# A two-layer encoder trunk: top-16 one-hot steps in quarters between the other tile's searches, V's first two places in a tile of their own, the shift's product behind a fourth block

## The chip, the cores and the metric

The program runs on one core of one Trainium2 chip. The metric is the device time of one execution in microseconds (us); the median of three executions of the kernel before is 1765.74 us (1764.5 to 1771.2). One execution was recorded by the hardware profiler: it took 1761.52 us, of which 1759.8 us lie between its first and its last instruction (the span).

The engines are TensorE (PE; its weight loads are PEld), VectorE (DVE), ScalarE (ACT), GpSimd (POOL) and SyncE (SP, which here only issues DMAs). Each engine takes its instructions in the order of its own queue.

## The reference, cut to what matters

Two layers work on 272 tokens (256 and 16 meta tokens) of width 1024. Each has a token mixer (a recurrent block, then a convolution block) and behind it the block that this change touches most, an expert retrieval:

```python
def peer_block(xc, w_query, sub_keys, expert_u, expert_v):
    q = (xc @ w_query).reshape(c, PEER_HEADS, 2, PEER_HALF)
    scores = jnp.einsum('chpk,pnk->chpn', q, sub_keys)          # 128 keys on each of 2 sides
    s1, i1 = lax.top_k(scores[:, :, 0], PEER_TOPK)               # 16 of 128
    s2, i2 = lax.top_k(scores[:, :, 1], PEER_TOPK)
    cand = (s1[..., :, None] + s2[..., None, :]).reshape(c, PEER_HEADS, 256)
    s, flat = lax.top_k(cand, PEER_TOPK)                         # 16 of 256
    idx1 = jnp.take_along_axis(i1, flat // PEER_TOPK, axis=-1)
    idx2 = jnp.take_along_axis(i2, flat % PEER_TOPK, axis=-1)
    expert = idx1 * PEER_N_KEYS + idx2
    g = jax.nn.softmax(s)
    act = gelu(einsum('chkd,cd->chk', expert_u[expert], xc))
    return einsum('chkd,chk->cd', expert_v[expert], g * act)
```

After each of the two, x becomes LayerNorm(alpha * x + f(x)).

## The kernel before, in words

**Most experts are computed densely.** For all but the last few tokens the kernel multiplies x by the whole of `peer_u` (128 places of 128 experts, one 512 KB tile each) and the weighted activations by the whole of `peer_v`, instead of gathering rows. A place's fp32 weights are split in two halves, hi (ACT, L155) and lo = raw - hi (L162), and PE makes 24 matmuls for it: 16 that read hi, then 8 that read lo. Weight tiles come from SP's queue four or five places ahead; hi and lo have two buffers each.

**U1** is the first half of U (places 0 to 63, `linears` with `u_store`). For the places below `LO_FROM` = 34, POOL makes lo; from place 34 on, DVE makes it. So in the first 34 places DVE is free for the top-k. **U2** is the second half, in which the one-hot products of the gate are made too; **V** is the third loop, over the 128 places of `peer_v`.

**The top-k** (`topk_steps`) of a tile of 128 tokens is a generator of DVE work. Its steps: 16 searches of 16 among 128 (each MAX8, MAX_INDEX, MATCH_REPLACE, MAX8, MAX_INDEX: L926 to L930); the 256 sums `cand` (L933); 8 searches among 256 (L941 to L945); conversions (`s`, `pu`, `pf`, L948 to L954); a one-hot `oh` by comparison (L961), its product with the indices (L967) and a sum (L970) that yields `idx`. Both layers have two tiles. The first, the late tokens, is run at once with its one-hot steps whole (one instruction of 4096 elements each). The second (`slow`) has its 24 searches run behind the first, and its remaining steps, in halves, go between places of U1 from 34 on. All that the searches issue stands in DVE's queue ahead of DVE's first lo. A scheduler may interleave independent searches; it does so in the kernel before.

**Gathered tokens.** For a few tokens the experts are gathered by index. SP writes their positions from the first tile's `idx` to DRAM (`few_spread`, at place `SPREAD` = 21) and reads them back four places later (`few_fetch`); DVE turns them into row numbers from place 35 on (`few_ids`).

**V's weights.** V's places come in groups of `JG` = 4. `weights` splits four places' activations (ACT L271, DVE L274) into a tile `w` that shares its two buffers (tag `xs`) with the x that U2 still reads, so the first group can be written only after U2's last matmul has read x. For the first group the split goes place by place.

**The end of layer 0's V** (`collect`) finishes eight output blocks one by one. From the first two finished blocks' sum PE makes a running mean (`shift`, L865, behind the third block), ACT copies it (L866), and DVE subtracts it from all blocks (L877), while the last weights' lo (L162), the sums and the squares for the LayerNorm go on.

Of the kernel before, what the change touches and what calls it, by code (L numbers as in the profile page):

```python
# [9 lines left out]
F32R = mybir.dt.float32r  # L10
# [3 lines left out]
OP = mybir.AluOpType  # L14
# [4 lines left out]
P = 128  # L19
# [4 lines left out]
T0 = SEQ + META  # L24
HEADS = 8
# [13 lines left out]
JG = 4  # L39
JA = 64  # L40
SPREAD = 21
WROW = 256
# [22 lines left out]
class Trunk:  # L65
# [489 lines left out]
    def peer(self, layer, n, xs):  # L555
# [10 lines left out]
        with tc.tile_pool(name=f"few{layer}", bufs=1) as kp:  # L566
# [5 lines left out]
            with tc.tile_pool(name=f"top{layer}", bufs=1) as sp:  # L572
# [9 lines left out]
                for c0, md in ctiles:  # L582
                    sc = sp.tile([P, 2 * HEADS, NK], F32, tag="sc", name="sc", bufs=2)
                    for g in range(4):
                        ps = self.psum("sps", (3, 4)).rearrange("p (a b) -> p a b", a=4)
                        for i in range(4):
                            b = 4 * g + i
                            nc.tensor.matmul(ps[:, i, :], q[:, b, c0:c0 + P], self.sk[:, 2 * layer + b % 2, :],  # L588
                                             start=True, stop=True)
                        nc.scalar.activation(sc[:, 4 * g:4 * g + 4, :], ps, AF.Copy)  # L590
                    if c0:
                        picked.append((c0, md, *self.topk(sp, sc, P)))
                        for few in early + late:
                            self.few_turn(sp, few, xs)
                        for few in early:
                            if few not in near:
                                self.few_topk(sp, few, q)
                    else:
                        slow = self.topk_steps(sp, sc, P, HEADS, 2)
                        for _ in range(3 * HEADS):  # L600
                            next(slow)
                        picked.append((c0, md))

                def u_store(j, ps):
# [32 lines left out]
                    if j == SPREAD + 4:  # L637
                        with tc.issue_after(self.last_load):
                            self.few_fetch(nc.sync, near, "pos")
                    if LO_FROM < j <= LO_FROM + len(near):  # L640
                        with tc.issue_after(self.dve_lo.ins):
                            self.few_ids(near[j - LO_FROM - 1], near[j - LO_FROM - 1]["pos"])
                    if t == len(picked) and not odd:
# [9 lines left out]
            with tc.tile_pool(name=f"act1{layer}", bufs=1) as ap1:  # L653
# [124 lines left out]

                def weights(j0, count):
                    t = self.xp.tile([P, JG * 2 * T0], F32R, tag="xs", name="w")  # L780
                    t = t[:, :JG * 2 * WROW].rearrange("p (j a n) -> p j a n", j=JG, a=2)
                    w = act_a[:, j0:j0 + count, :n] if j0 < JA else act_b[:, j0 - JA:j0 - JA + count, :n]
                    for s in ((slice(jj, jj + 1) for jj in range(count)) if j0 == 0 else (slice(0, count),)):
                        self.split_x(w[:, s], t[:, s, 0, :n], t[:, s, 1, :n])
                    return [t[:, jj] for jj in range(count)]

                half = NB // 2
# [60 lines left out]
    def collect(self, sp, acc, y, n):  # L848
        nc = self.nc
        ps, take, finish_block = acc  # L850
        self.tiles(sp, n)
        xr = [take(b) for b in range(4)]
        for b in range(NB):
            self.fifth = b < NB - 1
            finish_block(b)
            self.add_squares(n)
            if b < 4:
                with self.tc.issue_after(self.dve_lo.ins):
                    xr.append(take(4 + b))
            if b == 3:  # L860
                self.sum_rest(xr[4:])
            x, p_, z = xr[b], ps[b], y[:, b, :n]
            if b == 2:
                mu = self.bank(7, "shift")
                nc.tensor.matmul(mu[:, :n], self.fours, self.total, start=True, stop=True)  # L865
                nc.scalar.activation(self.shift, mu[:, :n], AF.Copy)  # L866
            if b >= 4:
                nc.vector.tensor_tensor(self.total, self.total, p_, op=OP.add)
            nc.vector.tensor_tensor(z, x, p_, op=OP.add)
            if 0 < b < 4:  # L870
                nc.vector.tensor_tensor(self.total, y[:, 0, :n] if b == 1 else self.total, z, op=OP.add)
# [36 lines left out]

    def topk(self, sp, sc, m):
        steps = self.topk_steps(sp, sc, m, HEADS)  # L910
        while True:
            try:
                next(steps)
            except StopIteration as done:
                return done.value

    def topk_steps(self, sp, sc, m, H, parts=1):
        nc = self.nc
        K = TOPK
        sv = sp.tile([P, H, 2, K], F32, tag=f"sv{H}", name="sv", bufs=1)  # L920
        si = sp.tile([P, H, 2, K], U32, tag=f"si{H}", name="si", bufs=1)
        for b in range(2 * H):
# [6 lines left out]
            nc.vector.max(v[:, 8:16], r[:m])  # L929
            nc.vector.max_index(i[:, 8:16], v[:, 8:16], r[:m])  # L930
            yield
# [5 lines left out]
        for h in range(H):  # L937
# [6 lines left out]
            nc.vector.max(v[:, 8:16], r[:m])  # L944
            nc.vector.max_index(i[:, 8:16], v[:, 8:16], r[:m])  # L945
            yield
# [6 lines left out]
        pf = sp.tile([P, 2 * H * K, 2], F16, tag=f"pf{H}", name="pf", bufs=1)  # L953
        nc.vector.tensor_copy(pf[:m], pu[:m].rearrange("p a n -> p (a n)")[:, :, None].to_broadcast([m, 2 * H * K, 2]))  # L954
        yield
# [4 lines left out]
        for g in range(0, 2 * H, w):  # L960
            nc.vector.tensor_tensor(oh[:m, g:g + w].rearrange("p g k (a b) -> p (g k) a b", b=2),  # L961
                                    self.iota16[:m].rearrange("p (a b) -> p a b", b=2)[:, None].to_broadcast(pairs),
                                    pf[:m, g * K:(g + w) * K, None, :].to_broadcast(pairs), op=OP.is_equal)
            yield
        for g in range(0, 2 * H, w):
            s = s16[:m].rearrange("p a h k -> p (a h) k")[:, g:g + w, None, :]
            nc.vector.tensor_tensor(oh[:m, g:g + w], oh[:m, g:g + w], s.to_broadcast([m, w, K, K]), op=OP.mult)  # L967
            yield
        for g in range(0, 2 * H, w):
            nc.vector.tensor_reduce(idx[:m].rearrange("p a h k -> p (a h) k")[:, g:g + w], oh[:m, g:g + w],  # L970
                                    op=OP.add, axis=AX.X)
            yield
# [428 lines left out]
```

## Time and profile before

| What | Value |
|---|---|
| median of three executions | 1765.74 us |
| the profiled execution | 1761.52 us, span 1759.8 us |
| ACT busy | 901.4 us, 51% of the span |
| DVE busy | 1512.1 us, 86% |
| POOL busy | 625.5 us, 36% |
| mean granted PE clock | 0.994 |
| HBM | 411.35 MB read, 240 GB/s over the span |

A busy time is the sum of an engine's instructions; an idle time stands in square brackets behind the instruction that ended it, with the engine and line that released it. Idle time of an engine that nobody waits for costs nothing. The rows that the argument rests on stand in the prediction.

### The profile page before, as it was taken

How to read it: one execution, taken by the hardware profiler on the slowest of the kernel's cores; microseconds unless marked ns; L12 is line 12 of the kernel's file. 1: busy time of each engine (PE TensorE's matmuls, PEld its weight loads, DVE VectorE, ACT ScalarE, POOL GpSimd, SP SyncE). 2: the span in 40 equal slices, each digit the busy share in tenths (PEclk: the TensorE clock that was granted, in tenths of full speed). 3: DMA queues.
4: the chain of work that ended last, by engine and by line, in shares of the span. 5: the costliest groups of instructions: out<-in, count | busy, mean ns of one | idle time of the engine just before them, and what ended most of it. 6: DMA issues, size and time to landing. Idle time of an engine off the chain costs nothing.

```text
span 1759.8 us, 34693 instructions
## 1 busy us (share of the span) xinstructions
PE 1716.6 (98%) x13436; PEld 1671.8 (95%) x13436; DVE 1512.1 (86%) x2821; ACT 901.4 (51%) x1489; POOL 625.5 (36%) x424
## 2 busy tenths in 40 slices
PE   8999999999999999999998999999999999999996
PEld 7899999999999999999887899999999999999996
DVE  7786998899997899988699769988889978889875
ACT  6554545554445455885532645445445455555552
POOL 1101992211202566752000017932102117777410
PEclk9999999999999999999999999999999999999998
DMA  5546667876757999999541356579767669999983
GB/s 204 168 139 175 183 210 266 300 230 192 229 182 253 329 369 367 361 353 331 163 135 60 117 168 178 185 254 324 235 193 231 199 197 326 344 360 347 349 305 123
DMA packets 126022, 423.83 MB, mean 241 GB/s; under 512 B 20768, under 2 KB 21920, under 8 KB 125728
## 3 DMA queue, kind: packets, MB, share of 16 engines
q1 hardware_dynamic: 96272, 324.04, 55.8%
q0 software_dynamic: 29584, 97.58, 15.1%
q8 instruction: 105, 1.72, 0.4%
q14 instruction: 61, 0.50, 0.1%
HBM read 411.35 MB, written 10.20 MB: 240 GB/s over the span
## 4 chain that ended last, share of the span: by engine, by line
PE 40%; DVE 8%; DMA 1%; issue 1%; ACT 1%; POOL 1%; POOLq 0%; ACTq 0%; DVEq 0%
PE u L190 20%; PE acc L772 11%; PE acc L776 7%; DVE cy L1281 2%; DVE odd L1281 2%; DMA rows<-peer_v,ids 1%; DMA own<-own 1%; DVE lo L162 1%; PE g L697 0%; PE g L698 0%; PE sps L588 0%; PE acc L812 0%; DVE x L373 0%; DVE x L337 0%; PE var L899 0%
## 5 line engine op out<-in xcount | busy, mean ns | idle before, releaser
L155 ACT ACTIVATE hi<-raw 128x1024 fp32r<-128x1024 f32 x556 | 588.5, 1059 | 563.4 <-PE acc L772 239.1
L162 DVE TENSOR_TENSOR lo<-raw,hi 128x1024 fp32r<-128x1024 f32 x488 | 595.6, 1222 | 142.0 <-ACT hi L155 140.1
L190 PE MATMUL u<-xs,hi 128*128 128x240 f32 (+2 forms) x4544 | 568.9, 277 | 2.0 <-ACT hi L155 1.4
L190 PEld LDWEIGHTS u<-xs,hi 128*128 128x128 f32 x4544 | 537.6, 189 | 3.1 <-ACT hi L155 1.6
L772 PE MATMUL acc<-w,hi 128*128 128x416 f32 (+1 forms) x1984 | 407.9, 347 | 2.5 <-DVE w L274 1.8
L772 PEld LDWEIGHTS acc<-w,hi 128*128 128x128 f32 x1984 | 345.3, 189 | 4.3 <-DVE w L274 2.2
L1066 POOL DMA_INDIRECT rows<-peer_v,ids x128 | 206.8, 1615 | 311.6 <-DVE few_out L1107 164.9
L190 PE MATMUL u<-xs,lo 128*128 128x240 f32 (+2 forms) x2272 | 307.9, 276 | 3.6 <-POOL lo L162 3.4
L190 PEld LDWEIGHTS u<-xs,lo 128*128 128x128 f32 x2272 | 280.6, 189 | 5.7 <-POOL lo L162 5.0
L776 PEld LDWEIGHTS acc<-w,lo 128*128 128x128 f32 x2048 | 266.9, 191 | 3.7 <-DVE lo L162 2.8
L776 PE MATMUL acc<-w,lo 128*128 128x208 f32 (+1 forms) x2048 | 268.1, 272 | 1.6 <-DVE lo L162 1.6
L162 POOL TENSOR_TENSOR lo<-raw,hi 128x1024 fp32r<-128x1024 f32 x68 | 176.8, 2619 | 103.2 <-ACT hi L155 64.7
L1107 DVE SCALAR_TENSOR_TENSOR few_out<-rows,act,few_out 128x1024 f32<-128x1024 f32 x120 | 153.7, 1281 | 13.4 <-DMA rows<-peer_v,ids 13.1
L1066 POOL DMA_INDIRECT rows<-u_rows,ids x48 | 61.5, 1281 | 177.0 <-DVE rows L1073 137.4
L1083 POOL DMA_INDIRECT act<-own,turn x80 | 113.6, 1420 | 27.5 <-issue 17.7
L226 PE MATMUL u<-x,raw 128*128 128x272 f32 x480 | 113.5, 396 | 5.2 <-DMA x<-h 5.2
L226 PEld LDWEIGHTS u<-x,raw 128*128 128x128 f32 x480 | 92.2, 192 | 24.3 <-DMA raw<-w_in 5.1
L704 ACT ACTIVATE act_b<-g 128x488 f32<-128x488 f32 (+39 forms) x50 | 19.4, 389 | 122.0 <-DVE act_b L666 99.3
L381 POOL TENSOR_SCALAR xs<-x,par 128x272 fp32r<-128x272 f32 (+1 forms) x4 | 3.5, 880 | 185.6 <-DVE x L373 185.6
L679 DVE TENSOR_TENSOR AB<-iota,iT 128x2048 f16<-128x2048 f16 x50 | 61.1, 1226 | 0.0
L1073 DVE SCALAR_TENSOR_TENSOR rows<-rows,wide 128x1024 f32<-128x1024 f32 x48 | 58.5, 1219 | 1.6 <-DMA rows<-u_rows,ids 1.4
L753 POOL COPY own<-act_b 128x512 f32<-128x512 f32 (+2 forms) x15 | 14.9, 1002 | 122.2 <-ACT act_b L715 94.8
(281 smaller groups left out, 1797.7 us busy)
## 6 DMA issues: line engine op xcount, KB each, us to landing
raw<-peer_u SPq DMA_DIRECT2D x256, 512.0 KB, 4.3
raw<-peer_v SPq DMA_DIRECT2D x248, 512.0 KB, 6.4
raw<-w_query SPq DMA_DIRECT2D x28, 512.0 KB, 3.6
raw<-pw SPq DMA_DIRECT2D x22, 512.0 KB, 3.5
raw<-w_in SPq DMA_DIRECT2D x16, 512.0 KB, 4.3
raw<-w_out SPq DMA_DIRECT2D x8, 512.0 KB, 4.1
raw<-peer_v SPq DMA_DIRECT2D x16, 256.0 KB, 4.2
own<-own POOLq DMA_DIRECT2D x15, 256.0 KB, 4.9
```

What stands on the lines that cost most here:

```text
L155: self.act_hi = nc.scalar.activation(hi, raw, AF.Copy).ins
L162: i = e.tensor_tensor(lo[:, s], raw[:, s], hi[:, s].bitcast(F32), op=OP.subtract)
L190: self.mm = nc.tensor.matmul(ps[:, :n], l[:, k, :], xs(k, r)[:, :n], start=start, stop=stop)
L226: self.mm = self.nc.tensor.matmul(ps[:, :n], raw[:, k, :], x[:, k, :n], start=k == 0, stop=k == NB - 1)
L679: nc.vector.tensor_tensor(AB.rearrange("p x c (a b) -> p (x c) a b", b=2), keys, iT[:, c0 // HC].rearrange("p x c b -> p (x c) b")[:, :, N ...
L772: self.mm = nc.tensor.matmul(acc[b][:, :2 * n].rearrange("p (a t) -> p a t", a=2), hi, w[:, :, :n], start=j == 0, stop=j == NK - JG - 1, s ...
L776: self.mm = nc.tensor.matmul(main[b][:, :n], hi if p_ else lo, w[:, i, :n], start=False, stop=j == NK - 1 and not p_, skip_group_check=True)
L1066: self.last_rows = self.nc.gpsimd.indirect_dma_start(out=t, out_offset=None, in_=table, in_offset=bass.IndirectOffsetOnAxis(ap=few["ids"][ ...
L1073: self.nc.vector.scalar_tensor_tensor(t, t, 1.0, few["x"], op0=OP.mult, op1=OP.mult, accum_out=few["act"][:, k:k + 1])
L1083: self.nc.gpsimd.indirect_dma_start(out=few["act"][:, k:k + 1], out_offset=None, in_=few["table"].rearrange("p j (t o) -> (p j t) o", o=1) ...
L1107: nc.vector.scalar_tensor_tensor(few["out"], t, w, few["out"], op0=OP.mult, op1=OP.add)
L1281: nc.vector.scalar_tensor_tensor(z, h, w, z, op0=OP.mult, op1=OP.add)
```

## The change

There are three edits, and two numbers that follow from the first.

1. **One-hot steps in quarters, between searches.** The first tile's generator is now made with `parts` = 4, so each of its three one-hot steps is four instructions of 1024 elements. A new function `interleave` runs the rest of it step by step and places, after its n-th step, the second tile's searches until 4n/3 (rounded down) are done; `issue_after(step)` fixes this order, and the same chain holds the second tile's remaining eight searches behind it. `SPREAD` goes from 21 to 32 and the row numbers are made from place 38 on.
2. **V's first two places** are split into a tile `first` of their own, so they no longer share a buffer with x.
3. **In `collect`** the product for `shift` is issued behind the fourth finished block, and the sums of blocks 2 and 3 follow it.

```diff
-SPREAD = 21
+SPREAD = 32
...
-                        picked.append((c0, md, *self.topk(sp, sc, P)))
+                        quick = self.topk_steps(sp, sc, P, HEADS, 4)
+                        for _ in range(3 * HEADS):
+                            next(quick)
...
                         slow = self.topk_steps(sp, sc, P, HEADS, 2)
-                        for _ in range(3 * HEADS):
-                            next(slow)
-                        picked.append((c0, md))
+                    picked.append((c0, md))
+                picked[0] += self.interleave(quick, slow, 2 * HEADS, 3 * HEADS)
...
-                    if LO_FROM < j <= LO_FROM + len(near):
+                    if 0 <= j - SPREAD - 6 < len(near):
...
-                def weights(j0, count):
-                    t = self.xp.tile([P, JG * 2 * T0], F32R, tag="xs", name="w")
+                def weights(j0, count, t=None):
+                    if t is None:
+                        t = self.xp.tile([P, JG * 2 * T0], F32R, tag="xs", name="w")
...
+                first = first_pool.__enter__().tile([P, 2, 2, n], F32R, name="first")
...
-                    w = weights(j, JG)
+                    w = weights(j, JG) if j else weights(0, 2, first) + weights(2, 2)
...
-            if b == 2:
+            if b == 3:
                 mu = self.bank(7, "shift")
...
-            if 0 < b < 4:
-                nc.vector.tensor_tensor(self.total, y[:, 0, :n] if b == 1 else self.total, z, op=OP.add)
+            if b == 1:
+                nc.vector.tensor_tensor(self.total, y[:, 0, :n], z, op=OP.add)
             if b == 3:
+                for i in (2, 3):
+                    nc.vector.tensor_tensor(self.total, self.total, y[:, i, :n], op=OP.add)
...
+    def interleave(self, steps, others, between, count):
+        step = result = None
+        done = turns = 0
+
+        def paced(one):
+            with self.tc.issue_after(step) if step else nullcontext():
+                next(one)
+            return self.step.ins
+
+        while result is None:
+            try:
+                step = paced(steps)
+            except StopIteration as end:
+                result = end.value
+                break
+            turns += 1
+            while done < min(between, 4 * turns // 3):
+                step = paced(others)
+                done += 1
+        for _ in range(count - done):
+            step = paced(others)
+        return result
```

What this does to the queues stands at three places. **First, DVE in layer 0's top-k, around the first tile's one-hot steps.** Before (`oh` is the one-hot tile, `sc`, `sv`, `si` scores, values and indices of the second tile's searches):

```order
L967 TENSOR_TENSOR oh<-oh,s_1817 128x4096
L926 MAX sv<-sc 128x8
L970 TENSOR_REDUCE idx<-oh 128x256
L927 MAX_INDEX si<-sv,sc 128x8
L928 MATCH_REPLACE r<-sv,sc 128x128
L926 MAX sv<-sc 128x8
L929 MAX sv<-r 128x8
L927 MAX_INDEX si<-sv,sc 128x8
L930 MAX_INDEX si<-sv,r 128x8
L928 MATCH_REPLACE r<-sv,sc 128x128
```

Now, at the first quarters:

```order
L978 CAST pf<-pu 128x512
L950 MAX sv<-sc 128x8
L951 MAX_INDEX si<-sv,sc 128x8
L952 MATCH_REPLACE r<-sv,sc 128x128
L953 MAX sv<-r 128x8
L954 MAX_INDEX si<-sv,r 128x8
L985 TENSOR_TENSOR oh<-iota_98,pf 128x1024
L950 MAX sv<-sc 128x8
L951 MAX_INDEX si<-sv,sc 128x8
```

The searches moved from behind the sum to between the quarters, and a search's five instructions, which were mixed with those of its neighbour, now stand one behind the other.

**Second, DVE at the end of the same stretch, just ahead of its first lo.** Before, then now (`cand`, `fv`, `fi` belong to the second tile's searches among 256):

```order
L943 MATCH_REPLACE r_2071<-fv,cand 128x256
L944 MAX fv<-r_2071 128x8
L945 MAX_INDEX fi<-fv,r_2071 128x8
L943 MATCH_REPLACE r_2077<-fv,cand 128x256
L944 MAX fv<-r_2077 128x8
L945 MAX_INDEX fi<-fv,r_2077 128x8
L162 TENSOR_TENSOR lo<-raw,hi 128x1024
```

```order
L965 MAX fv<-cand 128x8
L966 MAX_INDEX fi<-fv,cand 128x8
L967 MATCH_REPLACE r_2086<-fv,cand 128x256
L968 MAX fv<-r_2086 128x8
L969 MAX_INDEX fi<-fv,r_2086 128x8
L162 TENSOR_TENSOR lo<-raw,hi 128x1024
```

In both, the first lo stands behind the last search; nothing of the second tile's 24 searches moved behind it.

**Third, DVE in `collect`** (`xr` and `acc` are a block's two parts, `x` their sum). Before, then now:

```order
L871 TENSOR_TENSOR total<-x_10692 128x272
L869 TENSOR_TENSOR x_10692<-xr,acc_7259 128x272
L871 TENSOR_TENSOR total<-total,x_10692 128x272
L877 TENSOR_TENSOR x_10692<-x_10692,shift 128x272 x3
L877 TENSOR_TENSOR xr<-xr,shift 128x272 x3
L869 TENSOR_TENSOR x_10692<-xr,acc_7260 128x272
L877 TENSOR_TENSOR xr<-xr,shift 128x272
L871 TENSOR_TENSOR total<-total,x_10692 128x272
L873 SCALAR_TENSOR_TENSOR total<-shift,total 128x272
L877 TENSOR_TENSOR x_10692<-x_10692,shift 128x272
L874 TENSOR_TENSOR total<-total,rest 128x272
L162 TENSOR_TENSOR lo<-raw,hi 128x1024
```

```order
L878 TENSOR_TENSOR total<-x_10706 128x272
L876 TENSOR_TENSOR x_10706<-xr,acc_7268 128x272
L876 TENSOR_TENSOR x_10706<-xr,acc_7269 128x272
L162 TENSOR_TENSOR lo<-raw,hi 128x1024
L881 TENSOR_TENSOR total<-total,x_10706 128x272
L886 TENSOR_TENSOR x_10706<-x_10706,shift 128x272
```

The last lo, which stood behind all subtractions of the shift, now stands ahead of them.

More of the change, by code (lines that the diff above doesn't have):

```diff
@@ L639, in u_store @@
                             self.few_fetch(nc.sync, near, "pos")
[L640 removed]
+                    if 0 <= j - SPREAD - 6 < len(near):
                         with tc.issue_after(self.dve_lo.ins):
[L642 removed]
+                            self.few_ids(near[j - SPREAD - 6], near[j - SPREAD - 6]["pos"])
                     if t == len(picked) and not odd:
@@ L777, in v_mm @@
                                                        stop=j == NK - 1 and not p_, skip_group_check=True)
-                def weights(j0, count):
-                    t = self.xp.tile([P, JG * 2 * T0], F32R, tag="xs", name="w")
-                    t = t[:, :JG * 2 * WROW].rearrange("p (j a n) -> p j a n", j=JG, a=2)
+                def weights(j0, count, t=None):
+                    if t is None:
+                        t = self.xp.tile([P, JG * 2 * T0], F32R, tag="xs", name="w")
+                        t = t[:, :JG * 2 * WROW].rearrange("p (j a n) -> p j a n", j=JG, a=2)
                     w = act_a[:, j0:j0 + count, :n] if j0 < JA else act_b[:, j0 - JA:j0 - JA + count, :n]
-                    for s in ((slice(jj, jj + 1) for jj in range(count)) if j0 == 0 else (slice(0, count),)):
+                    for s in ((slice(jj, jj + 1) for jj in range(count)) if j0 < JG else (slice(0, count),)):
                         self.split_x(w[:, s], t[:, s, 0, :n], t[:, s, 1, :n])
                     return [t[:, jj] for jj in range(count)]
+                first_pool = tc.tile_pool(name=f"first{layer}", bufs=1, side="right", reuse_waits="tile")
+                first = first_pool.__enter__().tile([P, 2, 2, n], F32R, name="first")
                 half = NB // 2
@@ L929, in topk_steps @@
             nc.vector.max(v[:, 8:16], r[:m])
-            nc.vector.max_index(i[:, 8:16], v[:, 8:16], r[:m])
+            self.step = nc.vector.max_index(i[:, 8:16], v[:, 8:16], r[:m])
             yield
@@ L944, in topk_steps @@
             nc.vector.max(v[:, 8:16], r[:m])
-            nc.vector.max_index(i[:, 8:16], v[:, 8:16], r[:m])
+            self.step = nc.vector.max_index(i[:, 8:16], v[:, 8:16], r[:m])
             yield
@@ L953, in topk_steps @@
         pf = sp.tile([P, 2 * H * K, 2], F16, tag=f"pf{H}", name="pf", bufs=1)
-        nc.vector.tensor_copy(pf[:m], pu[:m].rearrange("p a n -> p (a n)")[:, :, None].to_broadcast([m, 2 * H * K, 2]))
+        self.step = nc.vector.tensor_copy(pf[:m], pu[:m].rearrange("p a n -> p (a n)")[:, :, None].to_broadcast([m, 2 * H * K, 2]))
         yield
@@ L960, in topk_steps @@
         for g in range(0, 2 * H, w):
-            nc.vector.tensor_tensor(oh[:m, g:g + w].rearrange("p g k (a b) -> p (g k) a b", b=2),
+            self.step = nc.vector.tensor_tensor(oh[:m, g:g + w].rearrange("p g k (a b) -> p (g k) a b", b=2),
                                     self.iota16[:m].rearrange("p (a b) -> p a b", b=2)[:, None].to_broadcast(pairs),
@@ L966, in topk_steps @@
             s = s16[:m].rearrange("p a h k -> p (a h) k")[:, g:g + w, None, :]
-            nc.vector.tensor_tensor(oh[:m, g:g + w], oh[:m, g:g + w], s.to_broadcast([m, w, K, K]), op=OP.mult)
+            self.step = nc.vector.tensor_tensor(oh[:m, g:g + w], oh[:m, g:g + w], s.to_broadcast([m, w, K, K]), op=OP.mult)
             yield
         for g in range(0, 2 * H, w):
-            nc.vector.tensor_reduce(idx[:m].rearrange("p a h k -> p (a h) k")[:, g:g + w], oh[:m, g:g + w],
+            self.step = nc.vector.tensor_reduce(idx[:m].rearrange("p a h k -> p (a h) k")[:, g:g + w], oh[:m, g:g + w],
                                     op=OP.add, axis=AX.X)
```

8 lines of the change are left out of this document (2 added, 6 removed).

## The prediction

> **What bounds the kernel.** I read the page first, then who PE waited for, then the timelines of the three places that the change touches.
>
> ```profile
> span 1759.8 us, 34693 instructions
> PE 1716.6 (98%) x13436; PEld 1671.8 (95%) x13436; DVE 1512.1 (86%) x2821; ACT 901.4 (51%) x1489; POOL 625.5 (36%) x424
> ```
>
> PE is the bound, at 98%. A change that leaves PE's work alone can gain only what PE idles, and every microsecond that PE is made to wait is lost. PE's waits that concern this change:
>
> ```profile
> PE u L190 <- POOL lo L162: 3.4, 3, 1.4
> PE acc L772 <- DVE w L274: 1.8, 2, 0.9
> PE shift L865 <- issue: 1.7, 1, 1.7
> ```
>
> These are total, count and longest: 6.9 us together, so without side effects the change is worth some 7 us of 1760, 0.4%. Now the engine that takes the rearranged work, over the top-k of layer 0 and of layer 1 (columns: PE, PEld, DVE, ACT, POOL busy):
>
> ```profile
> 172.00:265.00 93.00, 90.99 (x804) 90.22 (x804) 91.48 (x366) 47.09 (x71) 83.84 (x32) 1.00 0.63 191
> 1064.00:1157.00 93.00, 91.53 (x810) 90.76 (x809) 88.77 (x354) 46.23 (x69) 83.45 (x32) 1.00 0.61 187
> ```
>
> DVE is busy 91.48 and 88.77 of 93 us there. It must be done with the searches when place 34 asks for its first lo, so any DVE time that the change adds soon reaches PE.
>
> **The POOL stall that the quarters are to remove.** Layer 0, the whole one-hot steps on DVE, POOL's lo beside them, and PE:
>
> ```profile
> 211.65 4.30 DVE L961 TENSOR_TENSOR oh<-iota,pf 128x4096 f16<-128x4096 f16 x1
> 216.28 4.08 DVE L967 TENSOR_TENSOR oh<-oh,s 128x4096 f16<-128x4096 f16 x1
> 220.49 4.39 DVE L970 TENSOR_REDUCE idx<-oh 128x256 f32<-128x4096 f16 x1
> 276.60 1.22 DVE L961 TENSOR_TENSOR oh<-iota,pf 128x2048 f16<-128x2048 f16 x1
> 287.38 2.28 DVE L970 TENSOR_REDUCE idx<-oh 128x128 f32<-128x2048 f16 x1
> 211.40 2.41 POOL L162 TENSOR_TENSOR lo<-raw,hi 128x1024 fp32r<-128x1024 f32 x1 [0.28 <-ACT hi L155]
> 214.09 17.95 POOL L162 TENSOR_TENSOR lo<-raw,hi 128x1024 fp32r<-128x1024 f32 x6 [0.29 <-ACT hi L155]
> 218.26 1.17 PE L190 MATMUL u<-xs,lo 128*128 128x240 f32 x8
> 222.62 1.17 PE L190 MATMUL u<-xs,lo 128*128 128x240 f32 x8 [1.41 <-POOL lo L162]
> ```
>
> With POOL idle, half the size takes 1.22 us, so the whole needs some 2.15 (doubled, less the part that the next instruction overlaps). Beside POOL it takes 4.30: it starts at 211.65, while POOL's lo runs from 211.40 to 213.81, and it ends 2.14 us after that lo. So DVE waits for POOL's running lo to end, and POOL's next one waits for DVE: six take 17.95 instead of 14.4. The sum L970 (4.39 for 4096, as against 2.28 for half) does not show it. PE's two lo groups are 4.36 apart instead of a place's 2.70 (266.09 to 268.78 below), so this costs 1.7 us, a little more with the neighbours; I take 1.9 per layer.
>
> **Searches one behind the other.** A search that is mixed with its neighbour, then dependent instructions back to back:
>
> ```profile
> 226.50 0.28 DVE L926 MAX8 sv<-sc 128x8 f32<-128x128 f32 x1
> 227.67 0.27 DVE L926 MAX8 sv<-sc 128x8 f32<-128x128 f32 x1
> 242.67 0.27 DVE L928 MATCH_REPLACE8 r<-sv,sc 128x128 f32<-128x128 f32 x1
> 242.97 0.29 DVE L929 MAX8 sv<-r 128x8 f32<-128x128 f32 x1
> 243.30 0.09 DVE L930 MATCH_VALUE_LOAD si<-sv,r 128x8 f32 x1
> ```
>
> A mixed search costs 1.17 us (226.50 to 227.67) for five instructions, about 0.20 each and 0.06 for each load. Where one reads what the one right before it wrote, the step is 0.30 and 0.33 instead of 0.20. A search has three such links, so alone it costs about 1.17 + 0.40 = 1.57.
>
> **What DVE's queue becomes, layer 0:**
> - 16 searches alone: 16 x 0.40 = **+6.4**.
> - 8 searches among 256: 24 links instead of the 12 that stand so in the tail of the order before, at the same 0.13: **+1.6**.
> - 8 quarters that contend with POOL (four of L961, four of L967), each 0.55 of its own. After a quarter POOL starts a lo of 2.41. One search later (1.57) DVE asks again and waits 0.84; after two searches (3.14) POOL is in its second lo and DVE waits 1.7. By the 4n/3 rule six quarters follow one search and two follow two: 6 x 0.84 + 2 x 1.7 + 8 x 0.55 = 12.8, against 4.30 + 4.08 = 8.4: **+4.4**. The four sums stay at 4.4 in all.
> - The two `pu` conversions now have a MAX8 between them, so each can wait for a lo of its own: 0 to 2.4, I take **+1**.
>
> Together +13.4. From both sides: if no quarter ever waited, these would take 4.4 instead of 8.4 and DVE would come out at +5; if each waited a whole lo, at +24. The quarters' wait follows from the rows above, so I stay at **+13**. In layer 1 the two `pu` stand side by side as before: **+12**.
>
> **What that does to PE.** The end of the searches, the first lo (place 34), in layer 0 a later one, and PE's use of the lo, in each layer:
>
> ```profile
> 263.24 0.42 DVE L945 FIND_INDEX8 fi<-fv,r 128x8 uint32<-128x256 f32 x1
> 264.74 1.23 DVE L162 TENSOR_TENSOR lo<-raw,hi 128x1024 fp32r<-128x1024 f32 x1 [1.07 <-ACT hi L155]
> 278.15 1.23 DVE L162 TENSOR_TENSOR lo<-raw,hi 128x1024 fp32r<-128x1024 f32 x1 [0.33 <-ACT hi L155]
> 266.09 1.06 PE L190 MATMUL u<-xs,lo 128*128 128x240 f32 x8
> 268.78 1.06 PE L190 MATMUL u<-xs,lo 128*128 128x240 f32 x8
> 1152.05 0.42 DVE L945 FIND_INDEX8 fi<-fv,r 128x8 uint32<-128x256 f32 x1
> 1156.19 1.23 DVE L162 TENSOR_TENSOR lo<-raw,hi 128x1024 fp32r<-128x1024 f32 x1 [3.72 <-ACT hi L155]
> 1160.23 1.07 PE L190 MATMUL u<-xs,lo 128*128 128x240 f32 x8
> ```
>
> In layer 0 the searches end at 263.7 and PE uses that lo at 268.8. With +13 they end at 276.7, the lo at 277.9, so PE reads it 9.1 later than now: **+9.1**. In layer 1 they end at 1152.5 + 12 = 1164.5, the lo at 1165.7 instead of a use at 1160.2: **+5.5**. The POOL stalls that vanish ahead of place 34 (1.9 and 1.9) are no further gain: PE only reaches the wait earlier. Behind place 34 DVE still idles in a place (0.33 at 278.15), so it does not fall further behind, and does not give anything back either, since PE is the bound again.
>
> SP: the spread now stands ahead of the 34th weight tile and waits for `idx`, by the same count near 256 in layer 0. That load then comes some 6 us late, as the one at place 22 does now without a wait of PE, and its hi and lo would still be done before DVE's. Nothing added. The row numbers are made three places later, five places ahead of their first product: hidden.
>
> **The clock behind a long wait.** These are windows right behind a POOL stall and behind the two longest idle stretches of PE (the clock is the third column from the end):
>
> ```profile
> 223.00:226.00 3.00, 3.00 (x30) 3.00 (x29) 3.00 (x10) 1.36 (x3) 3.00 (x2) 1.00 0.00 0
> 970.00:975.00 5.00, 5.00 (x15) 3.35 (x14) 2.74 (x8) 2.71 (x8) 0.00 (x0) 0.58 0.00 0
> 864.00:866.00 2.00, 2.00 (x15) 2.00 (x14) 1.82 (x5) 1.32 (x4) 0.00 (x0) 0.74 0.54 217
> 866.00:868.00 2.00, 2.00 (x12) 2.00 (x11) 1.97 (x7) 2.00 (x5) 0.00 (x0) 0.50 0.00 0
> ```
>
> After 6.89 us idle the granted clock is 0.58 over 5 us (2.1 us lost), after 1.73 idle 0.74 and 0.50 over 2 us each (1.5 lost). After the POOL stall of 1.41 it stays 1.00. The new waits in front of place 34 are 11 and 7 us (9.1 and 5.5, and 1.9 each by which PE comes earlier), so I add **+1.7** in each layer, 3.4. The Trainium skill (TensorE: Matmul & The Clock Gate, Part 1) says that the clock falls to half after a window of about 3.4 us of idling and comes back after one of work; by it an estimate of 1.7 us is lost behind each long wait, which agrees, but the drop behind 1.73 us would not be expected, and there the rows decide.
>
> **V's first places:**
>
> ```profile
> 545.74 1.06 ACT L155 ACTIVATE hi<-raw 128x1024 fp32r<-128x1024 f32 x1 [1.31 <-PE u L190]
> 547.53 1.80 PE L772 MATMUL acc<-w,hi 128*128 128x416 f32 x8 [0.93 <-DVE w L274]
> 1439.51 1.66 PE L772 MATMUL acc<-w,hi 128*128 128x384 f32 x8 [0.90 <-DVE w L274]
> ```
>
> PE waits 0.93 (layer 1: 0.90) for the first w. With `first` ready early, it still needs this hi, which ends at 546.80, 0.2 behind the start of the wait: gain **0.7** per layer, **-1.4**. ACT and DVE do the same instructions a place earlier, where ACT idles for 1 to 2 us.
>
> **The shift:**
>
> ```profile
> 862.90 0.44 DVE L871 TENSOR_TENSOR total<-x 128x272 f32<-128x272 f32 x1
> 863.44 0.70 PE L865 MATMUL shift<-total,fours 128*128 128x272 f32 x2 [1.73 <-issue]
> 868.96 1.22 DVE L162 TENSOR_TENSOR lo<-raw,hi 128x1024 fp32r<-128x1024 f32 x1
> 870.24 0.48 PE L776 MATMUL acc<-w,lo 128*128 128x208 f32 x2 [0.69 <-DVE lo L162]
> ```
>
> PE waits 1.73 for the sum that DVE ends at 863.3. A block's 6 matmuls (0.7) now fill part of it, so about 1.0 is left. PE waits again at 870.24 for the last lo, which is now ahead of DVE's subtractions and can be done near 865. The least is 0.7, the most what lies between (0.7 + 0.7 + 1.5 of clock, and a share of DVE's 4 us): 4. I take **-2.5**; the squares, which come after the subtractions, set the end there.
>
> **Sum:** 9.1 + 5.5 + 3.4 - 1.4 - 2.5 = **+14.1 us**. Against the profiled execution, 1761.5, that is 1775.6; the median is 4.2 above that execution, so **1780 us**, 0.8% slower. A measurement of this kernel can tell about 0.5% (8.8 us) from no change.
>
> **Rivals.**
> - *The quarters slip between POOL's lo's, and DVE stays in time* (the change does what it is built for). Against it: DVE's 4.30 for 2.15 of work. The waits go: 3.8 of POOL, 1.4, 2.5: 7.7 less, **1758**. It decides if DVE's queue grows by less than 3.9 us in layer 0 (the 1.07 idle, and 2.8 between the lo's end at 265.97 and its use at 268.78). For it: the lower bound of +5 above comes near that. 8%.
> - *DVE grows by about half*: the links cost, the waits for POOL are half of mine, +8 and +7. PE loses 4 + 0.5 and some clock (2), and gains 3.9: **1768**, inside 0.5%. 17%.
> - *Each contention rounds up to one more lo of POOL* in both layers (2.4 + 0.3 each): **1785**, as the forecast otherwise. 15%.
>
> The rule behind the first and third is on a page, too: the Trainium skill (SBUF — State Buffer, Who interferes with whom) says that a DVE instruction with two SBUF inputs and a GpSimd one that reads SBUF lock each other out for a whole instruction, whoever starts first, and that a reduction never contends; the rows above agree (4.30 and 4.39). By that rule, more and shorter instructions mean more waits for a whole lo, which speaks against this change.
>
> **How the numbers follow.** The forecast (1780) 60%, the rivals 8, 17 and 15. The range reaches from the half case, less 2, to the rounded case, plus 2: 1766 to 1787. Slower by over 0.5%: 60 + 15, less 2 that falls inside: 0.73; within 0.5%: 17 + 2 and a share of the first rival: 0.21; faster: 0.06.
>
> **What would show it.** Right: PE waits in front of place 34 in both layers, for DVE lo, 11 and 7 us; the searches end near 277 and 1165; quarters at 0.6 to 2.3 us each; no POOL stall over 0.5; a clock near 0.6 behind those waits. Wrong: a first DVE lo that still waits for ACT hi, or quarters at 0.6 throughout. PE's waits for w and shift shrink in either case.

## The result and the profile after

The changed kernel takes **1775.49 us** (median of 8 runs, 1772.58 to 1778.99), the kernel before 1765.05 us beside it (8 runs). The ratio is 1.0060, 95% interval 1.0046 to 1.0075: slower by 10.4 us. The profiled execution has a span of 1775.1 us, 15.3 more than the one before; about 4 us of that is scatter of another stage, as the last experiment shows.

The page's first lines, and those of PE's waits that concern the change, by who ended them (total, count, longest, in us):

```profile
span 1775.1 us, 34708 instructions
PE 1720.1 (97%) x13436; PEld 1673.6 (94%) x13436; DVE 1527.7 (86%) x2839; ACT 901.0 (51%) x1489; POOL 613.4 (35%) x424
```

```profile
PE u L190 <- DVE lo L162: 14.4, 2, 8.5
PE shift L872 <- PE acc L777: 1.0, 1, 1.0
PE u L190 <- POOL lo L162: 0.6, 1, 0.6
```

The waits that the change was aimed at have shrunk: for POOL's lo 3.4 to 0.6, for V's first w 1.8 to nothing, for the shift 1.7 to 1.0. One row that was not there before is larger than all of them together: 14.4 us in two waits for DVE's lo. Both stand in front of place 34. The timeline of the changed kernel shows DVE's last search, its first lo, and PE, in layer 0 and then in layer 1 (start, duration, then in brackets the idle time before it):

```profile
275.57 0.42 DVE L969 FIND_INDEX8 fi<-fv,r 128x8 uint32<-128x256 f32 x1
275.91 1.21 DVE L162 TENSOR_TENSOR lo<-raw,hi 128x1024 fp32r<-128x1024 f32 x1
277.17 2.06 PE L190 MATMUL u<-xs,lo 128*128 128x240 f32 x8 [8.54 <-DVE lo L162]
279.03 2.98 PE L190 MATMUL u<-xs,hi 128*128 128x240 f32 x16
281.85 1.06 PE L190 MATMUL u<-xs,lo 128*128 128x240 f32 x8
282.75 1.96 PE L190 MATMUL u<-xs,hi 128*128 128x240 f32 x16
...
1173.45 0.42 DVE L969 FIND_INDEX8 fi<-fv,r 128x8 uint32<-128x256 f32 x1
1173.78 1.21 DVE L162 TENSOR_TENSOR lo<-raw,hi 128x1024 fp32r<-128x1024 f32 x1
1175.04 2.06 PE L190 MATMUL u<-xs,lo 128*128 128x240 f32 x8 [5.87 <-DVE lo L162]
1176.90 2.90 PE L190 MATMUL u<-xs,hi 128*128 128x240 f32 x16
```

The first lo has no bracket: hi was ready, and DVE came to it straight from the last search. Before, that lo still waited 1.07 us for ACT's hi. Behind the wait, 8 lo and 16 hi matmuls take 2.06 and 2.98 us instead of 1.06 and 1.96, which is a cost of its own. The granted clock (third column from the end) of these stretches:

```profile
277.00:279.00 2.00, 1.83 (x8) 1.83 (x9) 1.93 (x7) 1.06 (x1) 0.00 (x0) 0.50 0.31 70
279.00:283.00 4.00, 4.00 (x29) 4.00 (x28) 2.72 (x8) 1.32 (x2) 1.04 (x1) 0.73 0.77 244
1175.00:1177.00 2.00, 1.96 (x9) 1.96 (x10) 1.97 (x6) 1.06 (x1) 0.00 (x0) 0.50 0.41 98
```

Now what DVE does on the way there, in the timeline of layer 0: POOL's lo, quarters, and two searches of each kind that follow one another.

```profile
215.77 2.52 POOL L162 TENSOR_TENSOR lo<-raw,hi 128x1024 fp32r<-128x1024 f32 x1 [0.29 <-ACT hi L155]
217.53 1.31 DVE L985 TENSOR_TENSOR oh<-iota,pf 128x1024 f16<-128x1024 f16 x1
218.45 5.10 POOL L162 TENSOR_TENSOR lo<-raw,hi 128x1024 fp32r<-128x1024 f32 x2 [0.17 <-ACT hi L155]
221.90 2.20 DVE L985 TENSOR_TENSOR oh<-iota,pf 128x1024 f16<-128x1024 f16 x1
...
229.64 0.28 DVE L950 MAX8 sv<-sc 128x8 f32<-128x128 f32 x1
231.21 0.28 DVE L950 MAX8 sv<-sc 128x8 f32<-128x128 f32 x1
232.79 2.09 DVE L991 TENSOR_TENSOR oh<-oh,s 128x1024 f16<-128x1024 f16 x1
...
268.33 0.43 DVE L968 MAX8 fv<-r 128x8 f32<-128x256 f32 x1
270.57 0.43 DVE L968 MAX8 fv<-r 128x8 f32<-128x256 f32 x1
```

The quarter at 217.53 ends 0.55 us after POOL's lo (215.77 + 2.52 = 218.29): it waited 0.76 and then worked. A search among 128 takes 1.57 us from one MAX8 to the next, one among 256 takes 2.24. Grouped over the stretch from the first quarter to the end of the searches (behind the count the total in us and the mean in ns):

```profile
L985 DVE TENSOR_TENSOR oh<-iota,pf 128x1024 f16<-128x1024 f16 x4 | 6.3, 1568 | 0.0
L991 DVE TENSOR_TENSOR oh<-oh,s 128x1024 f16<-128x1024 f16 x4 | 6.0, 1504 | 0.0
L994 DVE TENSOR_REDUCE idx<-oh 128x64 f32<-128x1024 f16 x4 | 4.8, 1200 | 0.0
```

The eight quarters take 12.3 us where the two whole steps took 8.4 (4.30 + 4.08). The Trainium skill (SBUF — State Buffer, Who interferes with whom) says that a DVE instruction with two SBUF inputs and a GpSimd one that reads SBUF exclude each other for a whole instruction. The rows agree: each quarter ends about 0.55 us after a lo of POOL, and the sums, with one input, take 1.20 each beside the same POOL work.

The other two edits, in the changed kernel's timeline:

```profile
558.48 0.83 PE L773 MATMUL acc<-first,hi 128*128 128x416 f32 x3 [0.15 <-ACT tmp L719]
877.50 0.70 PE L872 MATMUL shift<-total,fours 128*128 128x272 f32 x2 [0.97 <-PE acc L777]
```

V's first wait fell from 0.93 to 0.15 in layer 0, and in layer 1 from 0.90 to nothing.

### The profile page after: what moved, and what is told of

It reads as the page before. It is cut to its first block, busy times and chain, and to the rows that moved or that the text cites. A ratio compares the mean times of both kernels' runs of the same rounds, so it can differ in the third digit from the quotient of the medians.

```text
span 1775.1 us, 34708 instructions
## 1 busy us (share of the span) xinstructions
PE 1720.1 (97%) x13436; PEld 1673.6 (94%) x13436; DVE 1527.7 (86%) x2839; ACT 901.0 (51%) x1489; POOL 613.4 (35%) x424
## 4 chain that ended last, share of the span: by engine, by line
PE 37%; DVE 13%; issue 1%; ACT 1%; POOLq 0%; POOL 0%; DVEq 0%; ACTq 0%
PE u L190 17%; PE acc L773 11%; PE acc L777 7%; DVE cy L1305 2%; DVE odd L1305 2%; DVE lo L162 1%; PE g L698 1%; PE g L699 1%; DVE si L954 1%; DVE si L951 1%; DVE r L952 0%; DVE sv L953 0%; DVE fi L969 0%; PE pre L246 0%; DVE fi L966 0%
## 5 line engine op out<-in xcount | busy, mean ns | idle before, releaser
L773 PE MATMUL acc<-w,hi 128*128 128x416 f32 (+1 forms) x1952 | 401.6, 347 | 1.6 <-ACT hi L155 1.1
L773 PEld LDWEIGHTS acc<-w,hi 128*128 128x128 f32 x1952 | 339.9, 189 | 3.4 <-ACT hi L155 1.5
L190 PE MATMUL u<-xs,lo 128*128 128x240 f32 (+2 forms) x2272 | 309.6, 278 | 15.1 <-DVE lo L162 14.4
L1090 POOL DMA_INDIRECT rows<-peer_v,ids x128 | 199.9, 1561 | 321.4 <-DVE few_out L1131 166.1
L777 PEld LDWEIGHTS acc<-w,lo 128*128 128x128 f32 x2016 | 261.9, 191 | 7.4 <-DVE lo L162 6.4
L777 PE MATMUL acc<-w,lo 128*128 128x208 f32 (+1 forms) x2016 | 264.4, 273 | 3.4 <-DVE lo L162 3.3
```

What stands on the lines that cost most here:

```text
L190: self.mm = nc.tensor.matmul(ps[:, :n], l[:, k, :], xs(k, r)[:, :n], start=start, stop=stop)
L773: self.mm = nc.tensor.matmul(acc[b][:, :2 * n].rearrange("p (a t) -> p a t", a=2), hi, w[:, :, :n], start=j == 0, stop=j == NK - JG - 1, s ...
L777: self.mm = nc.tensor.matmul(main[b][:, :n], hi if p_ else lo, w[:, i, :n], start=False, stop=j == NK - 1 and not p_, skip_group_check=True)
L1090: self.last_rows = self.nc.gpsimd.indirect_dma_start(out=t, out_offset=None, in_=table, in_offset=bass.IndirectOffsetOnAxis(ap=few["ids"][ ...
```

## The experiments

Stage lengths below are read from PE's timeline, from one marked matmul to another. "U1" here is the part of U1 in which the one-hot steps and place 34 lie: its first 57 places, from its first matmul to PE's first transpose of top-k results (`tps`). Before, it takes 156.62 us in layer 0 and 156.05 in layer 1, in the changed kernel 165.29 and 161.99.

### Which edit loses the time

**The kernel before with the two edits of V and of the shift only:** the top-k stays as it was.

```diff
+                first = first_pool.__enter__().tile([P, 2, 2, n], F32R, name="first")
...
-                    w = weights(j, JG)
+                    w = weights(j, JG) if j else weights(0, 2, first) + weights(2, 2)
...
-            if b == 2:
+            if b == 3:
...
```

> The kernel before with V's first two places in a tile of their own and the shift behind the fourth block; the one-hot steps stay whole. Theory (these two edits are gains, the loss is all in the top-k): PE waits 0.2 instead of 0.9 for the first w in both layers and the end of layer 0's V is 2.3 us shorter, so 3.7 us less than before, about 1761; no wait of PE for a DVE lo at place 34. Rival (one of these two edits is why PE waited 3.3 us in all for a DVE lo within layer 0's V after the change): V of layer 0 is some 4 us longer here too, and the kernel is no faster than before.

Measured: 1761.59 us against 1763.87 (12 and 23 runs), ratio 0.9987, interval 0.9973 to 1.0000. That is 2.3 us faster, with an interval that just reaches no change. Layer 0's V up to the shift takes 320.97 us here, 5 more than in the first profile of the kernel before, as the rival said; the last experiment finds nearly as much without any edit. U1 is as before (156.61 and 156.75), with POOL's stalls still in it:

```profile
PE u L190 <- POOL lo L162: 4.1, 4, 1.4
```

**The changed kernel without those two edits:** only the interleaving is left.

```diff
-                    w = weights(j, JG) if j else weights(0, 2, first) + weights(2, 2)
+                    w = weights(j, JG)
...
-            if b == 3:
+            if b == 2:
...
```

> The kernel before with the quarters between the searches alone (and the later spread). Theory: the whole loss is here: PE waits about 8.5 and 5.9 us for the first DVE lo of the two layers, and the time is that of the whole change plus the 3.7 us of the other two edits, 1779. Rival (the parts depend on one another): within 1 us of the whole change, 1775, or below.

Measured: 1782.58 us (4 runs) against 1763.87, ratio 1.0097, interval 1.0073 to 1.0120; 3.6 us more than expected. U1 takes 165.04 and 162.33, like the changed kernel's, and in front of place 34 PE waits 8.5 and 5.9 us for DVE's lo, as there:

```profile
PE u L190 <- DVE lo L162: 14.7, 3, 8.5
```

So the whole loss is in the interleaving, and the other two edits give a little back.

### The chain of searches, or the quarters

**The searches hang on the quarter only, not on one another.** The quarters stay where they are; between two quarters the scheduler is free to mix independent searches.

```diff
-                step = paced(others)
+                paced(others)
...
-            step = paced(others)
+            paced(others)
```

> The whole change, but each search is ordered behind the quarter only and no longer behind the search before it, so searches mix with their neighbours again; the quarters stay between them. Theory (back-to-back dependent searches make DVE late): two searches fit into one lo of POOL (2.34 against 2.41), a turn takes 2.96, DVE's searches end 8 us sooner, PE's waits in front of place 34 fall from 8.5 and 5.9 to 0.5 and 0, and with the clock 16 us go: about 1760. PE waits for POOL's lo 0.5 in place of 1.4. Rival (the waits of eight quarters for POOL make DVE late, however the searches stand): the quarters still take 1.3 to 2.2 each, PE's waits fall by 2 us each, about 1771.

Measured: **1755.77 us** against 1763.87, ratio 0.9948, interval 0.9932 to 0.9963. This is faster than both kernels, and 4 us under what was expected. U1 takes 154.96 and 154.15 us. The waits in front of place 34 are gone; the quarters (grouped), POOL's stalls, and the end of the searches in the timeline:

```profile
L985 DVE TENSOR_TENSOR oh<-iota,pf 128x1024 f16<-128x1024 f16 x4 | 6.4, 1601 | 0.0
L991 DVE TENSOR_TENSOR oh<-oh,s 128x1024 f16<-128x1024 f16 x4 | 5.8, 1451 | 0.0
```

```profile
PE u L190 <- POOL lo L162: 0.9, 2, 0.5
```

```profile
264.26 0.42 DVE L969 FIND_INDEX8 fi<-fv,r 128x8 uint32<-128x256 f32 x1
264.60 1.21 DVE L162 TENSOR_TENSOR lo<-raw,hi 128x1024 fp32r<-128x1024 f32 x1
```

The eight quarters cost 12.2 us here, as much as in the changed kernel (12.3). So they do not wait longer because the searches are chained; what went is, for the most part, the chain's own time. DVE is done 11.3 us earlier by the clock of the trace (264.68 against 275.99), 9.6 us earlier counted from U1's first matmul (172.27 and 174.01). Of these some 8 us are the searches; 1.2 are the sums `cand`, which took 2.27 us instead of 3.52.

**The one-hot steps whole, the chain kept:**

```diff
-                        quick = self.topk_steps(sp, sc, P, HEADS, 4)
+                        quick = self.topk_steps(sp, sc, P, HEADS)
```

> The changed kernel with the first tile's one-hot steps whole again (three instructions of 4096 elements), the searches still chained one behind the other. Theory (locks and chain add up): DVE's two whole steps take 8.4 us in place of the quarters' 12.3, so its searches end some 4.3 us earlier than in the changed kernel; POOL's stall of about 1.9 us per layer is back. PE's wait in front of place 34 falls from 8.5 to about 2.3 us in layer 0 and from 5.9 to nothing in layer 1: about 1764.5 us. Rival (only the quarters cost, the chain is harmless without them): no wait for DVE's lo in either layer, searches spaced 1.17 us, 1761. Second rival (the chain alone makes the loss): waits of 8.5 and 5.9 as now, 1775.

Measured: 1760.98 us against 1763.35 (10 and 20 runs), ratio 0.9978, interval 0.9968 to 0.9989. U1 takes 157.29 and 156.30. It came out 3.5 us under the theory, at the time that the first rival gave; PE's waits, and DVE and POOL in the timeline:

```profile
PE u L190 <- POOL lo L162: 3.6, 4, 1.4
PE u L190 <- DVE lo L162: 0.9, 2, 0.5
```

```profile
211.94 2.41 POOL L162 TENSOR_TENSOR lo<-raw,hi 128x1024 fp32r<-128x1024 f32 x1 [0.28 <-ACT hi L155]
213.44 3.06 DVE L985 TENSOR_TENSOR oh<-iota,pf 128x4096 f16<-128x4096 f16 x1
217.99 2.91 DVE L991 TENSOR_TENSOR oh<-oh,s 128x4096 f16<-128x4096 f16 x1
```

The two whole steps take 5.97 us, not the 8.4 that I had put in: the first asks 0.91 before POOL's lo ends (at 214.35), while in the kernel before it asked 2.16 before the end. How long a whole step waits is a matter of where POOL stands when DVE gets there. The searches end at 268.78, counted from U1's first matmul 4.6 us later than before, and PE waits only 0.5 us for it, in layer 0 (the other 0.4 of the row lie in layer 1, behind U1). So the second rival falls, and of the first the mechanism does: the chain does cost DVE its time without any quarters. But alone that time nearly fits in the room that DVE had, so that for PE it is close to harmless, as the first rival said.

**Halves, the chain kept:**

```diff
-                        quick = self.topk_steps(sp, sc, P, HEADS, 4)
+                        quick = self.topk_steps(sp, sc, P, HEADS, 2)
```

> The changed kernel with the first tile's one-hot steps in halves, the chain as it is. Theory (each locked instruction pays one wait of 0.8 to 1.7 us): four locked instructions of about 2.2 us, 8.8 us in place of 12.3, so PE's waits in front of place 34 fall to about 4 and 1.4 us, with about 1 us of POOL stall per layer: about 1768 us. Rival (DVE's loss to POOL depends on the elements and not on the number of instructions): the halves take 12 us together, the waits stay at 8.5 and 5.9, 1775.

Measured: 1763.48 us against 1763.35, ratio 1.0001, interval 0.9987 to 1.0014. U1 takes 160.51 and 156.24. The halves (grouped) and the waits:

```profile
L991 DVE TENSOR_TENSOR oh<-oh,s 128x2048 f16<-128x2048 f16 x2 | 4.5, 2234 | 0.0
L985 DVE TENSOR_TENSOR oh<-iota,pf 128x2048 f16<-128x2048 f16 x2 | 3.8, 1922 | 0.0
```

```profile
PE u L190 <- DVE lo L162: 3.7, 2, 3.2
PE u L190 <- POOL lo L162: 1.3, 3, 0.6
```

Four instructions cost 8.3 us and eight cost 12.3, so DVE's loss to POOL goes by the number of instructions and not by the elements; the rival falls. (Two whole ones cost 8.4 or 6.0: each instruction pays one wait, and how long that is depends on where POOL stands.) PE's wait in layer 0 is 3.2 where 4 was expected, in layer 1 it is 0.5 where 1.4 was expected. Behind the 3.2 us the clock falls, too:

```profile
272.01 1.16 PE L190 MATMUL u<-xs,lo 128*128 128x240 f32 x8 [3.17 <-DVE lo L162]
273.00 3.32 PE L190 MATMUL u<-xs,hi 128*128 128x240 f32 x16
```

```profile
274.00:276.00 2.00, 2.00 (x11) 2.00 (x11) 1.97 (x4) 0.00 (x0) 0.00 (x0) 0.50 0.67 211
```

The 16 hi matmuls take 3.32 us instead of 1.96. Behind the 0.5 us in layer 1 the clock stays at 1.00. The whole came out 4.5 us better than the theory's 1768; the waits are 1.7 us of that, and the rest stays open.

The runs side by side; the DVE column is the end of layer 0's searches, counted from U1's first matmul, against the kernel before:

| One-hot steps | Searches | Ratio | U1, layer 0 | U1, layer 1 | DVE, layer 0 |
|---|---|---|---|---|---|
| whole (before) | mixed | 1 | 156.62 | 156.05 | 0 |
| whole, with the V and shift edits | mixed | 0.9987 | 156.61 | 156.75 | 0 |
| whole | chained | 0.9978 | 157.29 | 156.30 | +4.6 |
| halves | chained | 1.0001 | 160.51 | 156.24 | +6.2 |
| quarters (the change) | chained | 1.0060 | 165.29 | 161.99 | +10.6 |
| quarters | mixed | 0.9948 | 154.96 | 154.15 | +1.1 |

All rows but the first have the V and shift edits, so the second is the one to compare with. With whole steps the chain costs nothing that shows (0.9978 against 0.9987), and with mixed searches the quarters gain (0.9948); only both together lose. DVE had 3.9 us of room in layer 0 (1.07 in front of its first lo, and 2.8 between that lo's end and its use). Up to there a later DVE costs PE nothing, from there on it costs PE the whole, and behind a long wait the clock on top. The room shrinks as POOL's stall does, since PE then comes to place 34 sooner: with whole steps +4.6 costs 0.5 us of waiting (room 4.1), with halves +6.2 costs 3.2 (room 3.0), with quarters +10.6 costs 8.5 (room 2.1).

### DVE's queue, or SP's

**POOL makes lo for five places more**, so that DVE's first lo is wanted some 13 us later. The spread of positions on SP's queue, which waits for the first tile's `idx`, stays in its place.

```diff
-DOTS_FROM, DOTS, ROWS, AHEAD, LO_FROM = 41, 14, 8, 2, 34
+DOTS_FROM, DOTS, ROWS, AHEAD, LO_FROM = 41, 14, 8, 2, 39
```

> The whole change with LO_FROM 39: POOL makes lo for five places more, so DVE's first lo is due 13.5 us later. Theory (DVE's queue is late, nothing else): PE's waits for a DVE lo in front of place 34 go in both layers, and the clock with them, 1757 to 1759; DVE's searches still end near 276. Rival (the spread of idx holds SP's queue and the weights of place 33 come late): a wait of several us stays at places 33 to 36, for ACT hi or POOL lo instead, 1768 or more.

Measured: 1759.77 us against 1763.87, ratio 0.9975, interval 0.9961 to 0.9989. U1 takes 156.51 and 154.94 us. DVE's searches end as late as in the changed kernel (102.1 us after U1's first matmul, there 102.0), but PE waits for nothing around places 34 to 39. The two waits for a DVE lo that it has lie further on, at 310 us and at 1190:

```profile
PE u L190 <- DVE lo L162: 2.1, 2, 1.5
```

So the loss hung on the point from which DVE is needed, and the later spread on SP's queue costs nothing that shows.

### The clock behind the wait

**Idle matmuls in front of place 34's lo products**, 32 in layer 0 and 20 in layer 1, whose result nobody reads; the lo products are ordered behind them:

```diff
...
+                    if i == 1 and (idle := self.feed.get(idx)):
+                        t = self.bank(5, "idle")
+                        for _ in range(idle):
+                            with tc.issue_after(self.mm.ins):
+                                self.mm = nc.tensor.matmul(t, self.ones16, self.ones16[:, None, :].to_broadcast([P, 4, P]),
+                                                           start=True, stop=True)
...
-                        mm(ps, hi, lo, i, k, i == 0 and k == 0, i == 1 and k == NB - 1)
+                        with tc.issue_after(self.mm.ins) if idle else nullcontext():
+                            mm(ps, hi, lo, i, k, i == 0 and k == 0, i == 1 and k == NB - 1)
...
+                self.feed = {LO_FROM: (32, 20)[layer]}
...
```

> The changed kernel with 32 (layer 0) and 20 (layer 1) idle matmuls in front of place 34's lo products, so that PE is busy while it waits for DVE's lo; nothing else is changed. Theory (a drop of the granted clock behind the wait is a cost of its own): the 8 lo and 16 hi matmuls behind the wait take 1.1 and 2.0 us in place of 2.1 and 3.0, granted clock 1.00 there, about 4 us less: 1771.5 us. Rival (another wait, such as the next place's lo, takes the clock's place): 1775.5.

Measured: 1768.93 us against 1763.35 (5 and 20 runs), ratio 1.0043, interval 1.0024 to 1.0061. U1 takes 163.42 and 160.50: 1.87 and 1.49 less than in the changed kernel, 3.4 us together. PE in layer 0, by the timeline, and the clock behind the wait:

```profile
267.21 7.08 PE L224 MATMUL idle<-ones 128*128 128x512 f16 x32
275.92 1.17 PE L192 MATMUL u<-xs,lo 128*128 128x240 f32 x8 [1.63 <-DVE lo L162]
276.93 1.95 PE L192 MATMUL u<-xs,hi 128*128 128x240 f32 x16
```

```profile
276.00:278.00 2.00, 2.00 (x18) 2.00 (x19) 1.93 (x6) 1.38 (x2) 0.00 (x0) 1.00 0.54 147
```

PE's first lo product starts at the same time as in the changed kernel (103.2 us after U1's first matmul in both), and PE goes on at full speed. So some 3.4 us of the loss was the clock, by the stage lengths. The two ratios, each to its own runs of the kernel before, say 3.0 us (1.0060 and 1.0043), but their intervals overlap (1.0046 to 1.0075 and 1.0024 to 1.0061), so the size rests on the stages.

### What varies by itself

The changed kernel's profile has two differences that the edits do not explain: layer 0's V, from its first matmul to the shift, took 320.27 us instead of 315.91, and the second half of U in layer 1, from the first one-hot product to V's first matmul, took 188.11 instead of 190.99 (0.9 of this is the wait for V's first w, which the edit removed). **The kernel before, unchanged, was profiled a second time.**

> The kernel before, profiled a second time. Theory (layer 0's V and layer 1's second half of U vary from execution to execution, as HBM is nearly full there): V of layer 0 takes another time than 315.9 us, anywhere from 316 to 322 as in the kernels of the other runs, and the PE wait of 1.4 us for ACT's hi in layer 1's U2 may be missing. Rival (the V and shift edits lengthen V by 3 to 5 us and shorten U2 by 2 to 3): V 315.9 within 0.5, U2 of layer 1 191.0 within 0.5, the wait of 1.4 there again.

Measured: 1764.23 us. V's first matmul, and the shift, in its timeline:

```profile
548.22 1.80 PE L772 MATMUL acc<-w,hi 128*128 128x416 f32 x8 [0.93 <-DVE w L274]
...
868.14 0.70 PE L865 MATMUL shift<-total,fours 128*128 128x272 f32 x2 [1.73 <-issue]
```

V takes 319.92 us here against 315.91 in the first profile of the same code, and the second half of U in layer 1 takes 189.34, without the 1.4 us of PE waiting for ACT's hi there. The waits in V, first profile and second:

```profile
PE acc L776 <- DVE lo L162: 1.6, 3, 0.7
```

```profile
PE acc L776 <- DVE lo L162: 4.4, 6, 1.5
```

So these differences come and go from one execution to the next. In the first profile the DMAs move 340 to 376 GB/s in six of eight stretches of V, and PE waits for a lo, or for another tile of DVE, in a few places that differ from run to run. What brings one of them on was not tried.

## Why the prediction was right, point by point

The sign, the place and the mechanism came out as forecast; the sizes were somewhat too large, which is why the median is 1775.5 and not 1780. (3.4 us of the difference are U1's growth, below; 0.7 is that the kernel before has a median of 1765.05 in 8 runs, not 1765.74.)

- **PE's waits.** Expected in front of place 34 in both layers, for DVE's lo, 11 and 7 us; measured there 8.5 and 5.9. The longest POOL stall left is 0.6 (0.5 was the limit named). The searches end at 275.99 and 1173.87; the 1165 that was named for layer 1 left out that U1 begins there 10.8 us later, of which 8.7 are U1's growth in layer 0.
- **DVE's growth** is the term that was mis-sized: +13.4 in layer 0 (used as 13), measured +10.6; +12 in layer 1, measured +10.6 too. By parts, in layer 0:

| Part | Said | Measured | From |
|---|---|---|---|
| 16 searches in a row | +6.4 | +5.2 | 1.52 each now, 1.20 before |
| 8 searches among 256 | +1.6 | +1.85 | 17.98 now, 16.13 before |
| quarters | +4.4 | +3.9 | 12.3 now, 8.4 before |
| `pu`, and all ahead of the first step | +1 | -0.3 | 40.56 - 1.52 now, 39.34 before |
| sums, `cand` | 0 | 0 | +0.4 and -0.4 |

The price of a chained search was right between two MAX8s (1.57; 1.52 in the mean). What I took too low was the search of before: 1.17 us is its steady state, but over all 16 it came to 1.20. I get it as 211.65 to 263.66, less the one-hot steps, `cand` and the wide searches, which leaves 19.19; in the same way 22.83 is left now for the 15 searches behind the first quarter. The second `pu` did wait for POOL, as said (2.08 us instead of 0.21), but the first one no longer did (0.21 instead of 1.30).
- **The quarters.** One search ahead: 0.84 + 0.55 = 1.39 said, 1.31 measured; two ahead: 2.25 said, 2.1 to 2.2 measured; six and two of them, as the 4n/3 rule gives. So a lock like this one can be worked out beforehand where order and phase are known. Where they move it cannot be: the whole steps of the chained kernel took 2.4 us less than I had put in, and single quarters with mixed searches took 0.67 to 2.83.
- **The clock.** Said 1.7 per layer. The rows behind the waits show 2.0 (1.00 + 1.02) in layer 0; feeding PE gave back 1.9 and 1.5. The 1.73 us at the shift, from which a part of the price came, is not PE's second longest wait before, as the prediction has it: the 5.16 us for the first load of x are longer, and the clock reads 1.00 behind them.
- **V's first places:** -0.7 per layer said; -0.8 and -0.9 measured at the wait.
- **The shift:** -2.5 said; the stage behind it went from 12.89 to 10.57 us, -2.3, of which about 0.7 is the block that now stands ahead of it, and the wait ahead of it fell from 1.73 to 0.97: -2.4 in all. The clock stays at 1.00 behind the shift. In the run of these two edits alone, the gain was 2.3 us where 3.9 had been said; the interval (0 to 4.8 us) holds both.
- **The sum.** U1 grew by 8.7 and 5.9 us (14.6), where 9.1 + 5.5 + 3.4 = 18.0 had been said. With the forecast's -3.9 for V and shift (by the rows -4.1) that is +10.7, and the median moved by +10.4. The difference of the two spans, 15.3, would have misled: 4.4 of it is V's scatter.
- **The rival that was built for** (the quarters slip in between and DVE stays in time, 1758) did not happen in this kernel, but it happens as soon as the chain is taken out: 1755.8. It was to decide at a growth of 3.9 us, and the kernels on both sides bear that out: +4.6 costs PE 0.5 us of waiting in layer 0, +6.2 costs 3.2, and +10.6 costs 8.5. I had counted the quarters' waits against that rival. They were there all the same, in full (12.2 us), and without the chain its time came out: the chain is the larger part (5.2 + 1.85). By these parts +3.6 would have been left; the +1.1 measured has two things more in it, `cand` (2.27 us instead of 3.92) and mixed searches at 1.12 us each instead of 1.20.
- **The other two rivals.** *DVE grows by about half* (+8 and +7, 1768) is about as near to DVE's measured growth (+10.6) as the forecast in layer 0, but not in layer 1, and its reason does not hold: the quarters added 3.9 of the 4.4 said, so their waits were not halved. *One more lo per contention* (1785) did not happen: no quarter here took more than 2.2 us.

## What to carry to other kernels

An order that is fixed to place one instruction also fixes everything that hangs on it: hold the step that has to be placed, and leave independent work behind it free to be mixed. Ahead of moving work onto an engine, work out its room as a number (here 3.9 us up to the first result that PE waits for), and add up all that the edit brings there, since two costs that each fit can miss together. Cutting an instruction into pieces to let another engine in multiplies the number of waits for that engine, and pays only as long as the engine that waits has room.

## What the runs showed of the hardware that was not expected

- The same code of V in layer 0 took 315.91 and 319.92 us in two executions of the kernel before, and between 317.2 and 322.5 in the others. A difference of a few microseconds in that stage, from one profile each, is no evidence of anything.
- A whole one-hot step took 4.30 us in one kernel and 3.06 in another, with the same work: the wait for POOL was 2.16 or 0.91, by where POOL's lo stood at that moment.
- Two DVE instructions of which the second reads what the first wrote are some 0.1 us further apart than independent ones (0.30 to 0.33 from start to start, not 0.20). On 16 searches that is 5 us of DVE, and the engine shows as nearly busy in both cases: from the first one-hot step to the end of the searches it idles 0.45 us before and 2.45 now, of some 7 that the chain costs. The rest is seen only in the starts of the rows.
- What a wait of PE costs in clock grows little with its length here: 1.5 to 1.7 us behind 1.73 (the shift, in two profiles of the kernel before), 1.8 behind 3.17 (the halves), 1.9 behind 5.87 and 2.0 behind 8.54. The shorter waits looked at, 0.5 to 1.64 us, left the clock at 1.00, that of 1.64 at the same shift in the kernel with the interleaving only. Where between them the drop begins, and why the 5.16 us at the start show none, is open.
